# Some weight tiles stay whole float32 and are multiplied in two passes, and one stage's activations are issued later

## The chip, the cores and the metric

The kernel runs on one core of a Trainium2 chip. The metric is the device time of one execution in microseconds (us). The kernel before took 2136.09 us (median of three runs, 2128.08 to 2136.28).

## The reference

Two transformer blocks run one after the other on 256 tokens of width 1024, all in float32. The first block has a mixer of causal pooling and a chunked state-space recurrence, the second a gated linear recurrence beside a short convolution. Each block ends in a product-key expert layer ("peer"), cut here to what is computed:

```python
q = (hf @ w_query).reshape(T, PEER_HEADS, 2, D_KEY // 2)
s1 = jnp.einsum("thk,hnk->thn", q[:, :, 0], sub_keys1)
v1, i1 = lax.top_k(s1, PEER_TOPK)            # the same for s2
cand = v1[..., :, None] + v2[..., None, :]
top_s, pos = lax.top_k(cand.reshape(T, PEER_HEADS, -1), PEER_TOPK)
gates = jax.nn.softmax(top_s, axis=-1)
u = expert_down[ib]; v = expert_up[ib]       # 16384 experts, 128 chosen per token
out = einsum("thk,thkd->td", gates * gelu(einsum("td,thkd->thk", hb, u)), v)
```

The first mixer projects the modulated norm of x with `w_in` (25 tiles of 128 columns), mixes, and projects back with `w_out` (12 tiles).

## The kernel before

Tokens lie along the free dimension: activations are tiles of 128 features by 256 tokens. A weight tile is 128 x 8 x 128 float32 (512 KB) and gives one 128 x 256 product by eight steps over k. All 645 weight tiles pass through one planned list (`plan`), and SyncE fetches them in that order (`fetch_to`, "raw", three buffers).

To keep float32 precision with TensorE's one-pass format (fp32r), a tile is split in two: ScalarE casts it to the high part (`high`, L90, "whi"), VectorE subtracts that from the raw tile for the low part (`low`, L97, "wlo"). Activations are split in the same way (hh and hl, yh and yl). A product (`product_steps`, L124 to L126) is then three one-pass matmuls for each k: hi·hh, hi·hl and lo·hh, 24 in all. `take` splits the tiles up to two ahead (PREP = 2) of the one that is multiplied. Where a plain float32 matmul is called for (small ones such as the gates, L889), the program makes two passes out of each call.

The program order is written out by hand, engine by engine, and each engine works in that order:

- The first mixer (to about 209 us) starts with the modulation: rows of `w_ada` are multiplied by the conditioning vector on VectorE (L313, "aw"), scaled into h (`scaled`), and the first two `w_in` products run as a `pair`. A loop over the other 23 `w_in` tiles (L716) evacuates each product (`evac`: convolution, gates, pooling), runs a piece of the recurrence, and multiplies one more `aw` row. Then come eight `w_outs` and four `w_outp` tiles (`out`, `both`), with the residual on VectorE.
- Each peer layer starts with routing (to about 382 us in the first): 34 "S" tiles of expert_down and 16 query tiles are multiplied on TensorE, and behind each, a fixed ration (DRIP) of top-16 searches is put on VectorE. 
- Then the one-hot stage (`ahead`, `one_hots`; 398 to 570 us): 46 further expert_down tiles are multiplied beside 64 groups of float16 matmuls (L1317) that spread the gates over the experts. `beside` pulls 5 or 6 of a product's eight steps per group. ScalarE makes the gelu of a product (L1261, L1266), casts the weight tiles (L90) and copies the spread gates out of PSUM (L1291, L1292).
- Then the expert_up stage (to about 895 us): TensorE alone multiplies without a break. The second mixer and the second peer layer follow in the same way.

Of the kernel before, what the change touches and what calls it, by code (L numbers as in the profile page):

```python
# [8 lines left out]
F32 = _mybir.dt.float32  # L9
# [42 lines left out]
class Net:  # L52
# [16 lines left out]
    def plan(self, key, index, eng=None, spare=False):  # L69
        self.items.append([key, index, eng, None, spare])  # L70

    def fetch_to(self, n):
        while self.fetched < min(n, len(self.items)):
            it = self.items[self.fetched]
            it[3] = self.stream.tile([128, KT, 128], F32, name="raw", bufs=RAW)
            self.nc.sync.dma_start(it[3], self.a[it[0]][it[1]])
            self.fetched += 1

    def high(self, n):
# [4 lines left out]
        self.fetch_to(n + 1)  # L84
        if it[4]:
# [7 lines left out]
    def low(self, n):  # L93
        it = self.items[n]
        if len(it[3]) == 3:
            raw, hi, lo = it[3]
            (self.nc.gpsimd if it[2] == "pool" else self.nc.vector).tensor_sub(lo, raw, hi.bitcast(F32))  # L97
            it[3] = hi, lo
# [35 lines left out]
    def proj(self, key, index, xh, xl):  # L134
# [94 lines left out]
    def norm_steps(self, x, r, g, shift, wk):  # L229
# [3 lines left out]
        for k in range(KT + 1):  # L233
            if k < KT:
                t = wk.tile([128, T], F32, name="nt", bufs=3)
# [128 lines left out]

    def plan_mixer1(self):
        for n, i in enumerate(self.M1):
            self.plan("w_in", i, eng=None)
        for f in range(0, 8, 2):
            self.plan("w_outs", f)
            self.plan("w_outs", f + 1)  # L370
            self.plan("w_outp", f // 2)

    def mixer1(self, constants):
        tc, nc, a = self.tc, self.nc, self.a
        with self.sbuf("m1") as m1, self.sbuf("w1", 2) as wk, self.psum("q1", 3) as self.pp, self.psum("p1", 3) as px:
            xs = m1.tile([128, 8, T], F32, name="xs")
            self.scratch_in(m1)
# [4 lines left out]
            with self.sbuf("early") as self.ap:  # L382
# [30 lines left out]
                h = {}  # L413

                def scaled(k):
# [4 lines left out]
                    h[k] = self.ap.tile([128, T], F32, name="nt4", bufs=4)  # L420
                    if k < 6:
                        nc.scalar.activation(self.hh[:, k], xs[:, k], AF.Identity, scale=g[:, k:k + 1],
                                             bias=m[:, k:k + 1])
                        nc.scalar.activation(h[k], xs[:, k], AF.Identity, scale=g[:, k:k + 1], bias=m[:, k:k + 1])
                    else:
                        nc.vector.tensor_scalar(h[k], xs[:, k], g[:, k:k + 1], m[:, k:k + 1], op0=ALU.mult,
                                                op1=ALU.add)
                        nc.scalar.copy(self.hh[:, k], h[k])

                def rest(k):  # L430
                    nc.vector.tensor_sub(self.hl[:, k], h.pop(k), self.hh[:, k].bitcast(F32))  # L431
# [3 lines left out]
                rests = {4: (0, 1), 5: (2, 3), 6: (4, 5), 7: (6, 7)}  # L435
# [3 lines left out]
                both = self.pair(first, [("w_in", i) for i in self.M1[:2]], self.hh, self.hl, prep=1)  # L439
                for f in range(KT):  # L440
                    self.add_sum(self.square(self.x[:, f]), f)
                for k in range(KT):
# [18 lines left out]
                    for f in rests.get(k, ()):  # L461
                        rest(f)
# [4 lines left out]
                for _ in both:  # L467
                    pass

# [20 lines left out]
            yh = m1.tile([128, 12, T], F32R, name="yh")  # L490
            yl = m1.tile([128, 12, T], F32R, name="yl")
# [114 lines left out]
            def outputs(p):  # L606
# [13 lines left out]
                def gated():  # L620
# [4 lines left out]
                    def parts():  # L625
                        self.add_square(y, p)

                        gn = self.v("ssd_norm", p)
# [27 lines left out]
            def pool_out():  # L656
# [3 lines left out]
                t = wk.tile([128, T], F32, name="po", bufs=3)  # L660
# [938 lines left out]
```

## Time and profile before

| | us |
|---|---|
| median of 3 runs | 2136.09 (2128.08 to 2136.28) |
| the profiled execution, its own time | 2142.61 |
| span of its trace, first to last instruction | 2140.8 |
| TensorE busy, VectorE busy, ScalarE busy | 1996.0, 1581.2, 1099.2 |
| mean granted TensorE clock | 0.982 |

PE is the matmul stream, PEld the weight load beside it, DVE is VectorE, ACT ScalarE, POOL GpSimd, SP SyncE. The entry of a matmul is longer than the distance to the next, as matmuls overlap: what a matmul costs in a stream is read from start to start. The same holds on DVE by a smaller amount.

### The profile page before, as it was taken

Reading aid. Unit: us, or ns where it says so; the run is one execution under the profiler, and the core shown is the slowest. Engines: PE = TensorE matmul, PEld = TensorE weight load, DVE = VectorE, ACT = ScalarE, POOL = GpSimd, SP = SyncE. Lnnn points to the kernel's source line nnn. Section 1 sums busy time; section 2 is a strip of 40 time slices with the busy share of each in tenths; the row PEclk is TensorE's granted clock in tenths of the full one; section 3 lists DMA queues with packets and bytes.
Section 4 is the critical chain, followed back from the end, with each engine's and each line's share of the span. In section 5 each row is a group of like instructions: output and inputs, shape, how many; then the busy total and the mean of one; then the engine's idle time right before and its main releaser. Section 6 shows DMA issues by size and latency. Waiting matters only on the chain.

```text
span 2140.8 us, 41974 instructions
## 1 busy us (share of the span) xinstructions
PE 1996.0 (93%) x16976; PEld 1959.5 (92%) x16976; DVE 1581.2 (74%) x3061; ACT 1099.2 (51%) x2019; POOL 53.2 (2%) x52
## 2 busy tenths in 40 slices
PE   4888888999999999999999998889999999999998
PEld 4778888888999999999999998888889999999998
DVE  7998899888755555675678779998887555555555
ACT  4564444665544444444466554446655444444444
POOL 3021000000000000000000010000000000000000
PEclk6999999999999999999999999999999999999999
DMA  6755444433455555575545564444335555555553
GB/s 249 254 185 181 148 157 149 149 129 129 159 206 187 187 187 187 192 247 192 187 149 178 182 208 153 148 148 146 132 129 182 192 188 183 191 183 186 186 187 127
DMA packets 102724, 376.68 MB, mean 176 GB/s; under 512 B 11648, under 2 KB 12032, under 8 KB 101504
## 3 DMA queue, kind: packets, MB, share of 16 engines
q1 hardware_dynamic: 101520, 369.38, 49.9%
q0 software_dynamic: 576, 4.19, 0.5%
q8 instruction: 133, 2.18, 0.4%
q14 instruction: 63, 0.52, 0.1%
q10 hardware_dynamic: 432, 0.41, 0.1%
HBM read 370.80 MB, written 3.15 MB: 175 GB/s over the span
## 4 chain that ended last, share of the span: by engine, by line
PE 69%; DVE 20%; ACT 5%; issue 3%; DMA 2%; SPq 0%; DVEq 0%; ACTq 0%
PE acc L1361 10%; PE acc L1363 10%; PE acc L1362 10%; PE mm L126 8%; PE mm L125 8%; PE mm L124 8%; DVE wlo L97 6%; PE acc L124 3%; PE acc L125 3%; PE acc L126 3%; ACT whi L90 2%; DVE aw L313 2%; DMA aw<-in_w_ada_dram 2%; PE mm L1317 2%; PE sm L1317 2%
## 5 line engine op out<-in xcount | busy, mean ns | idle before, releaser
L97 DVE TENSOR_TENSOR wlo<-raw,whi 128x1024 fp32r<-128x1024 f32 x642 | 785.6, 1225 | 256.6 <-ACT whi L90 255.2
L90 ACT CAST whi<-raw 128x1024 fp32r<-128x1024 f32 x642 | 671.9, 1048 | 178.9 <-PE acc L1362 97.4
L126 PE MATMUL mm<-hh,wlo 128*128 128x256 f32 x2120 | 604.1, 285 | 38.7 <-DVE wlo L97 38.7
L124 PE MATMUL mm<-hh,whi 128*128 128x256 f32 x2120 | 604.6, 285 | 11.5 <-ACT whi L90 8.9
L125 PE MATMUL mm<-hl,whi 128*128 128x256 f32 x2120 | 600.0, 283 | 10.9 <-DVE hl L431 6.0
L1361 PE MATMUL acc<-wh,whi 128*128 128x256 f32 x2048 | 575.1, 281 | 2.9 <-DVE x L1471 2.1
L1362 PE MATMUL acc<-wl,whi 128*128 128x256 f32 x2048 | 574.1, 280 | 1.9 <-DVE wl L117 1.7
L1363 PE MATMUL acc<-wh,wlo 128*128 128x256 f32 x2048 | 573.5, 280 | 2.2 <-DVE wlo L97 2.2
L126 PEld LDWEIGHTS mm<-hh,wlo 128*128 128x128 f32 x2120 | 407.7, 192 | 48.5 <-DVE wlo L97 48.1
L124 PEld LDWEIGHTS mm<-hh,whi 128*128 128x128 f32 x2120 | 404.8, 191 | 15.4 <-ACT whi L90 10.1
L125 PEld LDWEIGHTS mm<-hl,whi 128*128 128x128 f32 x2120 | 406.3, 192 | 12.7 <-DVE hl L431 6.5
L1361 PEld LDWEIGHTS acc<-wh,whi 128*128 128x128 f32 x2048 | 385.9, 188 | 3.3 <-DVE x L1471 2.3
L1363 PEld LDWEIGHTS acc<-wh,wlo 128*128 128x128 f32 x2048 | 386.4, 189 | 2.6 <-DVE wlo L97 2.6
L1362 PEld LDWEIGHTS acc<-wl,whi 128*128 128x128 f32 x2048 | 385.0, 188 | 2.7 <-DVE wl L117 2.7
L116 ACT CAST wh<-X 128x256 fp32r<-128x256 f32 x256 | 103.4, 404 | 231.2 <-PE acc L1363 231.2
L124 PE MATMUL acc<-hh,whi 128*128 128x256 f32 x736 | 215.9, 293 | 0.0
L125 PE MATMUL acc<-hl,whi 128*128 128x256 f32 x736 | 205.0, 279 | 0.0
L126 PE MATMUL acc<-hh,wlo 128*128 128x256 f32 x736 | 204.5, 278 | 0.0
L117 DVE TENSOR_TENSOR wl<-X,wh 128x256 fp32r<-128x256 f32 x256 | 108.1, 422 | 90.9 <-ACT wh L116 90.9
L124 PEld LDWEIGHTS acc<-hh,whi 128*128 128x128 f32 x736 | 139.0, 189 | 0.0
L125 PEld LDWEIGHTS acc<-hl,whi 128*128 128x128 f32 x736 | 138.8, 189 | 0.0
L126 PEld LDWEIGHTS acc<-hh,wlo 128*128 128x128 f32 x736 | 138.3, 188 | 0.0
(345 smaller groups left out, 1970.4 us busy)
## 6 DMA issues: line engine op xcount, KB each, us to landing
raw<-in_down_dram SPq DMA_DIRECT2D x256, 512.0 KB, 3.2
raw<-in_up_dram SPq DMA_DIRECT2D x256, 512.0 KB, 3.8
raw<-in_w_in_dram SPq DMA_DIRECT2D x81, 512.0 KB, 3.3
aw<-in_w_ada_dram SPq DMA_DIRECT2D x48, 512.0 KB, 4.5
raw<-in_w_query_dram SPq DMA_DIRECT2D x32, 512.0 KB, 3.3
raw<-in_w_outs_dram SPq DMA_DIRECT2D x8, 512.0 KB, 3.8
raw<-in_w_out_dram SPq DMA_DIRECT2D x8, 512.0 KB, 4.1
raw<-in_w_outp_dram SPq DMA_DIRECT2D x4, 512.0 KB, 3.7
```

The costliest lines, as they stand in the source:

```text
L90: self.nc.scalar.copy(hi, it[3])
L97: (self.nc.gpsimd if it[2] == "pool" else self.nc.vector).tensor_sub(lo, raw, hi.bitcast(F32))
L116: self.nc.scalar.copy(hi, src)
L117: self.nc.vector.tensor_sub(lo, src, hi.bitcast(F32))
L124: nc.tensor.matmul(ps, hi[:, k], xh[:, k], start=k == 0 and clear, stop=False, skip_group_check=True)
L125: nc.tensor.matmul(ps, hi[:, k], xl[:, k], start=False, stop=False, skip_group_check=True)
L126: nc.tensor.matmul(ps, lo[:, k], xh[:, k], start=False, stop=k == KT - 1, skip_group_check=True)
L313: self.nc.vector.scalar_tensor_tensor(w, w, 1.0, self.crow, op0=ALU.mult, op1=ALU.mult, accum_out=self.mod[:, j:j + 1])
L1317: nc.tensor.matmul(pg[:, j], o2[j], o1[:, j // 2, b, :, j % 2], start=b == 0, stop=b == 1, skip_group_check=True)
L1361: nc.tensor.matmul(o, hi[:, d], wh, start=i == 0 and d < 4, stop=False, skip_group_check=True)
L1362: nc.tensor.matmul(o, hi[:, d], wl, start=False, stop=False, skip_group_check=True)
L1363: nc.tensor.matmul(o, lo[:, d], wh, start=False, stop=i == NK - 1, skip_group_check=True)
```

## The change

1. A planned tile can be "whole": `high` and `low` pass it by, and `product_steps` calls eight plain float32 matmuls of the raw tile with a float32 activation, two passes each. Whole tiles come from a ring of three buffers of their own ("rawf") or from the ring of the others ("shared").
2. In the first mixer, `w_in` tiles number 0, 1, 2, 4, 6, ... 16 in the order of multiplication (10 of 25) and all 12 output tiles are whole. The activations are kept in float32 (h and ys); hh and hl are made after the first pair, yh and yl are gone.
3. In each routing, ten S tiles (5, 8, ... 32) are whole. `norm_steps` also writes a float32 h, in the first peer layer with one more ScalarE instruction for each k.
4. In the one-hot stage, the gelu of a product is issued after step 3 of the next product, where it stood right behind its own.

```diff
@@ fetch_to, high
+            if it[2] == "own":
+                it[3] = self.whole.tile([128, KT, 128], F32, name="rawf", bufs=RAW)
+            else:
+                it[3] = self.stream.tile([128, KT, 128], F32, name="raw", bufs=RAW)
...
+        if it[2]:
+            it[3] = it[3],
+            return
@@ product_steps
-        hi, lo = self.take(key, index, prep)
+        w = self.take(key, index, prep)
+        if len(w) == 1:
+            for k in range(KT):
+                nc.tensor.matmul(ps, w[0][:, k], xh[:, k], start=k == 0 and clear, stop=k == KT - 1,
+                                 skip_group_check=True)
+                yield
+            return
+        hi, lo = w
@@ norm_steps
+                t = wk.tile([128, T], F32, name="nt", bufs=3) if whole is None or shift is not None else whole[:, k]
...
+                    if whole is not None:
+                        nc.scalar.activation(whole[:, k], t, AF.Identity, bias=shift[:, k:k + 1])
@@ plan_mixer1
+        return n < 2 or n % 2 == 0 and n < 18
...
-            self.plan("w_in", i, eng=None)
+            self.plan("w_in", i, whole=self.unsplit(n) and "own")
...
+            self.plan("w_outs", f, whole="own")
+            self.plan("w_outs", f + 1, whole="shared")
+            self.plan("w_outp", f // 2, whole="own" if f % 4 else "shared")
@@ mixer1, modulation
-                both = self.pair(first, [("w_in", i) for i in self.M1[:2]], self.hh, self.hl, prep=1)
+                both = self.pair(first, [("w_in", i) for i in self.M1[:2]], h, None, prep=1)
...
-                    for f in rests.get(k, ()):
-                        rest(f)
...
+                for k in range(KT):
+                    nc.scalar.copy(self.hh[:, k], h[:, k])
+                for k in range(KT):
+                    nc.vector.tensor_sub(self.hl[:, k], h[:, k], self.hh[:, k].bitcast(F32))
@@ mixer1, recurrence
-                        nc.scalar.mul(yh[:, 4 + p], y, gn)
-                        post.append(lambda: nc.vector.scalar_tensor_tensor(
-                            yl[:, 4 + p], y, gn, yh[:, 4 + p].bitcast(F32), op0=ALU.mult, op1=ALU.subtract))
+                        nc.scalar.mul(ys[:, 4 + p], y, self.v("ssd_norm", p))
@@ mixer1, output
-                        nc.tensor.matmul(o, hi[:, kk], yh[:, k], start=False, stop=False, skip_group_check=True)
-                        nc.tensor.matmul(o, hi[:, kk], yl[:, k], start=False, stop=False, skip_group_check=True)
-                        nc.tensor.matmul(o, lo[:, kk], yh[:, k], start=False, stop=k == 3, skip_group_check=True)
+                        nc.tensor.matmul(ps[f][:, 1], w[:, 4 * b + k], ys[:, k], start=False, stop=k == 3,
+                                         skip_group_check=True)
@@ plan_peer, peer
+                self.plan(down, st[1], whole=4 < st[1] < N0 and st[1] % 3 == 2 and "own")
...
+                return self.proj(down, i, *([h] if self.items[self.taken][2] else [self.hh, self.hl]))
@@ peer, one-hot stage
+                            for k, _ in enumerate(product(ps, i, clear=slot < 4)):
+                                if k == 3 and done:
+                                    activated(*done)
+                                yield
+                            done = kind, i, ps, o
+                        activated(*done)
```

VectorE in the loop over the `w_in` tiles, before: "wlo" is the subtraction for a weight tile, "cva" the convolution, "xs" its gate, "aw" a modulation row.

```order
111 L97 TENSOR_TENSOR wlo<-raw,whi 128x1024
112 L359 SCALAR_TENSOR_TENSOR cva<-mm,hcw,cva 128x255
...
115 L679 SCALAR_TENSOR_TENSOR xs<-th,cva 128x256
116 L313 SCALAR_TENSOR_TENSOR aw,mod<-aw,crow 128x1024
117 L97 TENSOR_TENSOR wlo<-raw,whi 128x1024
118 L359 SCALAR_TENSOR_TENSOR cva<-mm,hcw,cva 128x255
...
121 L679 SCALAR_TENSOR_TENSOR xs<-th,cva 128x256
122 L547 TENSOR_TENSOR cbt<-aux,U 128x512
123 L313 SCALAR_TENSOR_TENSOR aw,mod<-aw,crow 128x1024
124 L97 TENSOR_TENSOR wlo<-raw,whi 128x1024
```

The same place now (every line of the program has another number, as the file grew).

```order
104 L103 TENSOR_TENSOR wlo<-raw,whi 128x1024
105 L374 SCALAR_TENSOR_TENSOR cva<-mm,hcw,cva 128x255
...
108 L682 SCALAR_TENSOR_TENSOR xs<-th,cva 128x256
109 L560 TENSOR_TENSOR cbt<-aux,U 128x512
110 L328 SCALAR_TENSOR_TENSOR aw,mod<-aw,crow 128x1024
111 L374 SCALAR_TENSOR_TENSOR cva<-mm,hcw,cva 128x255
...
114 L682 SCALAR_TENSOR_TENSOR xs<-th,cva 128x256
...
117 L328 SCALAR_TENSOR_TENSOR aw,mod<-aw,crow 128x1024
118 L103 TENSOR_TENSOR wlo<-raw,whi 128x1024
```

Between the two `aw` rows the subtraction is gone; it stands in every second turn of the loop.

ScalarE in the one-hot stage, before: "X<-acc" and "act<-acc" are the two halves of a gelu, "X<-mm" and "X<-sm" the copies of spread gates, "whi" the cast of a weight tile.

```order
325 L1214 ACTIVATE oh_4682<-cst,kI_2199 128x128 x2
326 L1261 ACTIVATE X_2466<-acc_2203 128x236
327 L1266 ACTIVATE act<-acc_2203 128x20
328 L90 CAST whi<-raw 128x1024
329 L1291 ACTIVATE X_2466<-sm 128x26x4
330 L1292 ACTIVATE X_4413<-sm 128x64x4
```

The same stage now.

```order
312 L1211 ACTIVATE oh_4188<-cst,kI_1734 128x128 x2
313 L96 CAST whi<-raw 128x1024
314 L1297 ACTIVATE X_2010<-sm 128x24x4
315 L1298 ACTIVATE X_3757<-sm 128x64x4
316 L1211 ACTIVATE oh_4188<-cst,kI_1734 128x128 x2
317 L1259 ACTIVATE X_2010<-acc_1737 128x216
318 L1264 ACTIVATE act<-acc_1737 128x40
```

The cast stands ahead of the gelu of the product before it, and the copies of a group can come ahead of that gelu.

## Rows read from the trace of the kernel before

**Rows 1.** Windows by stage: us; PE, PEld, DVE, ACT, POOL busy; clock; DMA, GB/s

```profile
0.00:47.00 47.00, 18.83 (x90) 16.53 (x91) 36.35 (x82) 19.67 (x38) 18.86 (x15) 0.66 0.73 268
47.00:139.00 92.00, 83.11 (x658) 76.55 (x658) 87.84 (x172) 56.31 (x122) 2.31 (x4) 0.97 0.65 236
139.00:167.00 28.00, 18.83 (x139) 17.38 (x138) 26.30 (x46) 11.23 (x22) 10.19 (x9) 0.88 0.37 132
167.00:209.00 42.00, 35.31 (x291) 33.92 (x291) 38.05 (x80) 19.16 (x33) 8.73 (x8) 1.00 0.47 168
240.00:382.00 142.00, 124.96 (x1014) 120.96 (x1013) 141.04 (x479) 62.42 (x101) 0.00 (x0) 0.98 0.43 149
398.00:570.00 172.00, 158.19 (x1533) 153.48 (x1532) 144.73 (x262) 106.49 (x292) 0.00 (x0) 1.00 0.38 132
1284.00:1430.00 146.00, 126.07 (x1043) 121.62 (x1043) 139.96 (x483) 65.52 (x106) 0.00 (x0) 1.00 0.43 151
1640.00:2120.00 480.00, 480.00 (x4078) 480.00 (x4077) 278.57 (x346) 228.76 (x340) 0.54 (x1) 1.00 0.55 188
```

**Rows 2.** TensorE timeline: start, us, line, operation, idle; split products at the two clocks

```profile
1111.95 0.28 PE L126 MATMUL mm<-hh,wlo 128*128 128x256 f32 x1
...
1113.90 0.28 PE L125 MATMUL mm<-hl,whi 128*128 128x256 f32 x1
...
37.60 0.41 PE L125 MATMUL mm<-hl,whi 128*128 128x256 f32 x1
...
41.23 0.41 PE L124 MATMUL mm<-hh,whi 128*128 128x256 f32 x1
```

**Rows 3.** The gates' plain float32 matmuls (L889): one chain, then all 32 passes

```profile
1114.47 1.03 PE L889 MATMUL aux<-xc,wg 128*128 128x256 f32 x4
...
L889 PE MATMUL aux<-xc,wg x32: 378/379/454, 1110.8 to 1137.0; 128*128 128x256 f32 x32
```

**Rows 4.** VectorE timeline, one turn of the `w_in` loop

```profile
76.15 1.22 DVE L97 TENSOR_TENSOR wlo<-raw,whi 128x1024 fp32r<-128x1024 f32 x1
77.28 1.51 DVE L359 SCALAR_TENSOR_TENSOR cva<-mm,hcw,cva 128x255 f32<-128x255 f32 x3
...
79.04 1.22 DVE L313 SCALAR_TENSOR_TENSOR aw<-aw,crow 128x1024 f32<-128x1024 f32 x1
...
80.19 1.22 DVE L97 TENSOR_TENSOR wlo<-raw,whi 128x1024 fp32r<-128x1024 f32 x1
```

**Rows 5.** VectorE timeline, the end of the modulation

```profile
29.57 1.73 DVE L97 TENSOR_TENSOR wlo<-raw,whi 128x1024 fp32r<-128x1024 f32 x1
...
45.82 0.98 DVE L431 TENSOR_TENSOR hl<-nt,hh 128x256 fp32r<-128x256 f32 x2
...
49.65 0.48 DVE L359 SCALAR_TENSOR_TENSOR cva<-mm,hcw,cva 128x255 f32<-128x255 f32 x1 [2.52 <-ACT cva L357]
```

**Rows 6.** VectorE timeline, the end of the recurrence

```profile
162.68 0.48 DVE L630 SCALAR_TENSOR_TENSOR yl<-yo,vecs,yh 128x256 fp32r<-128x256 f32 x1
163.08 0.41 DVE L666 TENSOR_TENSOR yl<-po,yh 128x256 fp32r<-128x256 f32 x1
```

**Rows 7.** TensorE timeline: the first output product behind the pair, the next norm's sum

```profile
166.75 0.36 PE L758 MATMUL mm<-yh,whi 128*128 128x256 f32 x1
...
207.46 0.61 PE L224 MATMUL sm<-ones,ns 128*128 128x1 f32 x4 [1.62 <-POOL ns L219]
```

**Rows 8.** Waits in 240 to 382, then 1290 to 1440: us, times, longest

```profile
PE mm L126 <- DVE wlo L97: 15.9, 16, 1.9
...
PE mm L126 <- DVE wlo L97: 18.0, 17, 1.9
```

**Rows 9.** Waits in 398 to 570, the first one-hot stage

```profile
ACT X L1261 <- PE acc L126: 40.8, 27, 2.5
...
PE sm L1317 <- ACT X L1292: 6.3, 12, 0.9
...
PE mm L1317 <- ACT X L1292: 5.1, 9, 0.9
```

More of the change, by code (lines that the diff above doesn't have):

```diff
@@ L66, in psum, with plan @@
         return self.tc.tile_pool(name=name, bufs=bufs, space=PSUM, reuse_waits="tile")
-    def plan(self, key, index, eng=None, spare=False):
-        self.items.append([key, index, eng, None, spare])
+    def plan(self, key, index, whole=False, spare=False):
+        self.items.append([key, index, whole, None, spare])
     def fetch_to(self, n):
@@ L227, in total_sum, with norm_steps @@
         return ps
-    def norm_steps(self, x, r, g, shift, wk):
+    def norm_steps(self, x, r, g, shift, wk, whole=None):
         nc = self.nc
@@ L749, in out @@
                 q = ps[f] = self.pp.tile([128, 2, T], F32, name="mm")
-                self.product(q[:, 0], "w_outs", f, yh[:, 4:], yl[:, 4:])
+                self.product(q[:, 0], "w_outs", f, ys[:, 4:], None)
             def both(j):
-                hi, lo = self.take("w_outp", j)
+                w, = self.take("w_outp", j)
                 for b in range(2):
@@ L795, in mixer1 @@
                 ps[f] = self.pp.tile([128, 2, T], F32, name="mm")
-            two = self.pair([ps[0][:, 0], ps[1][:, 0]], [("w_outs", 0), ("w_outs", 1)], yh[:, 4:], yl[:, 4:])
+            two = self.pair([ps[0][:, 0], ps[1][:, 0]], [("w_outs", 0), ("w_outs", 1)], ys[:, 4:], None)
             for _ in range(KT - 2):
@@ L1063, in S @@
             def S(i):
-                return self.proj(down, i, self.hh, self.hl)
+                return self.proj(down, i, *([h] if self.items[self.taken][2] else [self.hh, self.hl]))
             with self.sbuf("rt") as rt:
+                self.whole = rt
+                h = rt.tile([128, KT, T], F32, name="h")
                 kt = rt.tile([128, 16, 128], F32, name="keys")
@@ L1118, in peer @@
                 nc.sync.dma_start(kt, a[keys])
-                norm = self.norm_steps(self.x, row, g, shift, rt)
+                norm = self.norm_steps(self.x, row, g, shift, rt, h)
                 next(norm)
@@ L1250, in product, with activated @@
                             yield
+                    def activated(kind, i, ps, o):
+                        nonlocal there
+                        if kind == "H":
+                            held[i] = ps
+                        elif kind == "R":
+                            acts[i] = o
+                            nc.scalar.activation(o, ps, gelu)
+                        else:
+                            t1 = t0 + 4 if t0 else 0
+                            nc.scalar.activation(o[:, t1:], ps[:, t1:], gelu)
+                            if not t0:
+                                there += 1
+                                return
+                            t = og.tile([128, 192], F32, name="act", bufs=2)[:, :t1]
+                            nc.scalar.activation(t, ps[:, :t1], gelu)
+                            first.append((t1, o[:, :t1], t))
```

79 lines of the change are left out of this document (19 added, 60 removed).

## The prediction

> **What bounds the kernel now.** I read the windows by stage first [rows 1], since the mean over the span says little here: TensorE is busy 480.00 of 480 us in the second expert_up stage, and there no tile changes. The changed stages look different. In the loop of the first mixer (47 to 139 us) VectorE is busy 87.84 of 92 us, in the two routings 141.04 of 142 and 139.96 of 146. TensorE is behind it there: the waits say that in the routings it stood still for a weight tile's low part 15.9 and 18.0 us [rows 8]. VectorE is the bound of these stages, and the subtraction for a weight tile is a large part of its work: one turn of the loop is 4.04 us from one subtraction to the next, of which the subtraction takes 1.13 (76.15 to 77.28) [rows 4]. In the one-hot stage neither is full (TensorE 158.19 and VectorE 144.73 of 172 us) [rows 1]; ScalarE waits there 40.8 us for the product whose gelu is next, and TensorE in turn 6.3 + 5.1 us for ScalarE's copies [rows 9].
>
> **What a whole tile costs.** A split product runs 17 steps in 1113.90 - 1111.95 = 1.95 us, 0.1147 each, so 24 take 2.75 us [rows 2]. A plain float32 matmul is two passes; four of them span 1.03 us, the last one's own entry is 0.378, so three steps take 0.65: 0.217 each [rows 3]. A whole tile has 16: 3.47 us, 0.72 more than a split one. It saves VectorE 1.13 us, and ScalarE the cast. So it is a trade of 1.13 on one engine against 0.72 on another, and pays only where VectorE is the one that is late. No stretch of 16 passes stands in the trace: from below I bound a pass by 0.1147 (it can't be shorter than a one-pass matmul), from above by its whole entry, 0.378; I take 0.217, the nearest row, of the same shape.
>
> The Trainium skill's "FP8 and Floating Point Precision", section "TensorE Precision Notes", speaks against the change: true float32 takes four passes through the array. By that, 32 passes stand against 24, and a whole tile would be 4/3 of 2.75, 3.67 us, an estimate; the trace shows two entries, each of nearly twice a one-pass matmul [rows 2, 3], so 3.8 rather than four. By the page the ten output tiles below would take 2 us more, and the sum would be 2094.
>
> **The first mixer, step by step.**
> Modulation (to 47 us). Three subtractions go (the first took 1.73 us, the others 1.1 each) and eight of hl, two of which have an entry of 0.98 us, move behind the pair; the last h can so be ready about 6 us earlier, and the loop's first convolution, which waited 2.52 us until 49.65 [rows 5], follows it. The moved hl work fills that idle time. Against it stands the clock: it was 0.66 in this stage [rows 1], and at the lower of the two levels, 1.2 GHz, the same 17 steps took 41.23 - 37.60 = 3.63 us, almost twice as long [rows 2]; a whole tile is then some 6.6 us instead of 3.5, and tile 2 may run so. I take -5, with -2 and -7 as ends.
>
> Loop (47 to 139 us). Whole tiles 4, 6, ... 16 take away seven subtractions: 7 x 1.13 = -7.9. TensorE gets 7 x 0.72 = 5 us more; its 658 instructions at 0.1147 make 75 of 92 us, so 17 were free and it stays behind VectorE. -8.
>
> End of the recurrence (139 to 167 us). Three subtractions for output tiles go (3.4 us) and twelve of yl: eight at 0.40 (162.68 to 163.08) and four at 0.34, 4.6 us [rows 6]. VectorE was busy 26.30 of 28 us, but TensorE and GpSimd (busy 18.83 and 10.19 us) [rows 1] hand it the last products, the pooling and the sum of squares here, and one of these can be late next. Of 8.0 I take -6, the ends -4 and -8.
>
> Output tiles (167 to 209 us). Here the trade turns. From the first product behind the pair (166.75) to the next norm's sum (207.46) [rows 7] are 40.7 us, with ten products: 27.5 us of TensorE before, 34.7 now. Nine subtractions (10.2 us) leave VectorE's 38.05, so TensorE becomes the bound: 34.7, the spread norm 0.5 and the residual, its square and GpSimd's addition behind the last product, some 4 us, make about 40. I take 0, with +4 and -3 as ends. Taking their turn here are also the fetches: a whole tile's buffer comes free when TensorE has read it, not when VectorE has, and SyncE's later fetches (the next query tiles) queue behind that. Six tiles are in flight, some 20 us, and the DMA engines were 0.47 busy [rows 1], so I price this at nothing; with less cover it would show as ScalarE waiting for raw tiles.
>
> Norm before the first routing: eight more ScalarE instructions of about 0.3 us in a chain that TensorE waits for: +1 (0 to 2.5).
>
> **The routings.** Ten subtractions less in each is 11.3 us on VectorE; TensorE gets 7.2 us more and loses at most its waits for low parts, 15.9 and 18.0 [rows 8], a net 8.7 and 10.8. As both engines end up nearly level and the ration of searches is uneven from step to step, neither limit is reached: -8 each, ends -3 and -11.
>
> **The one-hot stages.** ScalarE no longer stands before an unfinished product, where the copies and the cast queued up behind its gelu and TensorE behind the copies. What TensorE lost to that is 11.4 us in the first stage [rows 9]. The cast is now immediately ahead of the gelu, and a group that ends between them waits for both, so I count half: -5 each, ends 0 and -11. VectorE, at 144.73 of 172 us [rows 1], allows it.
>
> Sum: -5 - 8 - 6 + 0 + 1 - 16 - 10 = -44 us. From the profiled execution's own 2142.61 that is 2098.6; that execution lies 6.5 us above the median of the runs, 2136.09, so I forecast 2092.
>
> **Rivals.**
> TensorE takes over in the routings too. For it: its need there, 142 - 15.9 + 7.2 = 133.3 us, against VectorE's 141.0 - 11.3 = 129.7: it is already the larger. Against it: it has two split tiles of lead over VectorE. If unevenness eats most of the gain (-2 each) and the output tiles cost 4: -44 + 12 + 4 = -28, 2108.
> The delayed gelu brings nothing: the stall moves from the gelu to the cast. For it: ScalarE's work in a group is the same, 106.49 us in 172 [rows 1]. Then -34: 2102.
> VectorE stays the bound all through: the whole 11.3 twice, 8 in the recurrence, 11 in each one-hot stage: about -69, 2067.
> Slower: in a long stream of plain passes the weight load isn't hidden, and a pass costs its whole entry, 0.378 [rows 3]. A whole tile is then 6.05 us, 3.3 above a split one. The routings would get 33 us more on TensorE, which had 17 to spare (142 - 124.96) [rows 1]: +16 each; the ten output tiles 60.5 and a tail of 4 against 40.7: +24; the loop 23 against 17 spare: +6; with -5 and -10 as before, +47: 2183. It decides from about 0.27 a pass on, where the routings stop gaining. Against it: chains of four already run at 0.217.
>
> **How the numbers follow.** 0.5% of 2136, 11 us, is what a measurement of this kernel can tell from no change. The forecast gets 0.50, TensorE in the routings 0.22, of which 0.05 for a gain under 11 us, the useless delay 0.15, VectorE throughout 0.06, slower 0.05, and 0.02 that some wait I don't see eats it all. So faster 0.88, the same 0.07, slower 0.05. The good ends of the terms together with VectorE throughout give about 2066, the bad ends without the slower case (-2, -8, -4, +4, +2, -6, 0) make -14, 2122; as they won't all fall together I take 2068 to 2116.
>
> **What would show it.** The plain products should step at 0.217. The subtractions for weight tiles should number 42 fewer; 47 to 139 us should shrink by about 8 and TensorE's wait for low parts in the routings to a few us, while VectorE falls below 0.97 busy there. In the one-hot stage ScalarE's wait for the product should be mostly gone and TensorE's for the copies halved. Were a routing not shorter by at least 3 us, or the output tiles longer by more than 5, the forecast would be wrong in that step.

## The result: 57 us less, and the profile after

| | before | after |
|---|---|---|
| median (lowest to highest) of 4 runs each, us | 2132.19 (2128.08 to 2136.28) | 2074.80 (2073.15 to 2077.16) |
| ratio, with its 95% interval | | 0.9725 (0.9704 to 0.9746) |
| the profiled execution, its own time | 2142.61 | 2077.16 |
| span of its trace | 2140.8 | 2075.4 |

The change is worth 57 us by the medians and 65 us between the two profiled executions. The 8 us between these are not the change's: the profiled execution of before lies 10 us above the median of its runs, that of after 2 us.

To see where the time went I took the same pieces of work in both traces as landmarks and compared the time between them: the first convolution of the loop on VectorE, the VectorE instruction that reads a norm's sum ("re"), the first and the last score of a routing on TensorE, the transpose of the chosen keys behind it, the first and the last group of spread gates, SyncE's last store.

```
stretch                                     before    after     step    forecast
start to the first convolution               49.65    44.19     -5.5       -5
  to the norm's sum behind the recurrence   117.27   103.61    -13.7    -8 and -6
  to the next norm's sum (output tiles)      42.13    39.85     -2.3        0
  to the first score of routing 1            23.55    24.38     +0.8       +1
routing 1, to the last score                125.62   119.09     -6.5   }
  from there to the keys                     22.36    17.94     -4.4   }   -8
  to the first group of gates                10.23    10.96     +0.7
one-hot stage 1, first to last group        168.96   158.20    -10.8       -5
expert_up 1, to the second mixer's norm     521.2    517.7      -3.5        0
second mixer and its output                 213.6    214.2      +0.6        0
routing 2, to the last score                126.38   119.50     -6.9   }
  from there to the keys                     22.29    17.93     -4.4   }   -8
  to the first group of gates                10.22    10.96     +0.7
one-hot stage 2                             169.01   158.19    -10.8       -5
expert_up 2, to the last store              515.42   515.41      0.0        0
```

The windows after, cut at the same pieces of work as [rows 1] (us; PE, PEld, DVE, ACT, POOL busy; clock; DMA, GB/s):

```profile
0.00:42.00 42.00, 20.98 (x86) 17.20 (x87) 31.67 (x73) 15.83 (x35) 17.89 (x15) 0.72 0.75 282
42.00:122.00 80.00, 78.35 (x539) 69.64 (x538) 76.52 (x157) 45.22 (x104) 2.22 (x2) 1.00 0.76 277
122.00:148.00 26.00, 23.00 (x165) 20.56 (x164) 23.55 (x45) 10.30 (x25) 10.82 (x11) 1.00 0.43 156
148.00:188.00 40.00, 40.00 (x207) 35.91 (x206) 28.11 (x72) 11.07 (x24) 7.98 (x8) 1.00 0.51 180
212.00:350.00 138.00, 133.73 (x984) 128.83 (x985) 133.98 (x492) 56.81 (x101) 0.00 (x0) 0.98 0.44 157
367.00:528.00 161.00, 156.16 (x1534) 152.57 (x1532) 143.35 (x261) 106.11 (x294) 0.00 (x0) 1.00 0.41 142
1238.00:1378.00 140.00, 132.69 (x994) 127.59 (x993) 132.41 (x486) 55.67 (x97) 0.00 (x0) 0.99 0.47 168
```

In the loop (42 to 122 us) and the routings TensorE and VectorE are now equally full; in the output stage (148 to 188) TensorE is busy 40.00 of 40 us and VectorE only 28.11, where VectorE was the fuller [rows 1].

A whole tile costs what the four-pass chain [rows 3] had told. Two of the long streams on TensorE's timeline (start, us, line, operation):

```profile
151.60 3.62 PE L131 MATMUL mm<-ys,rawf 128*128 128x256 f32 x16
233.69 3.62 PE L131 MATMUL mm<-h,rawf 128*128 128x256 f32 x16
```

Sixteen passes span 3.62; without the last one's own entry, 0.378, fifteen steps take 3.24: 0.216 each, 3.46 us a tile. The weight loads are hidden, so the slower rival has no ground.

VectorE in the loop, where [rows 4] had a subtraction in every turn:

```profile
67.48 1.22 DVE L328 SCALAR_TENSOR_TENSOR aw<-aw,crow 128x1024 f32<-128x1024 f32 x1
...
68.63 1.51 DVE L374 SCALAR_TENSOR_TENSOR cva<-mm,hcw,cva 128x255 f32<-128x255 f32 x3
...
70.39 1.22 DVE L328 SCALAR_TENSOR_TENSOR aw<-aw,crow 128x1024 f32<-128x1024 f32 x1
...
71.53 1.22 DVE L103 TENSOR_TENSOR wlo<-raw,whi 128x1024 fp32r<-128x1024 f32 x1
72.67 1.51 DVE L374 SCALAR_TENSOR_TENSOR cva<-mm,hcw,cva 128x255 f32<-128x255 f32 x3
```

A turn without a subtraction goes from `aw` to `aw` in 70.39 - 67.48 = 2.91 us, and no row has an idle time before it: VectorE sets the pace of this turn. The end of the modulation, to be set beside [rows 5]:

```profile
40.19 2.76 DVE L483 TENSOR_TENSOR hl<-ys,hh 128x256 fp32r<-128x256 f32 x8
...
44.19 1.00 DVE L374 SCALAR_TENSOR_TENSOR cva<-mm,hcw,cva 128x255 f32<-128x255 f32 x2 [0.91 <-ACT cva L372]
```

The eight moved hl instructions stand where VectorE had waited 2.52 us; 0.91 us of waiting is left, and the convolution is 5.5 us earlier. No run takes back the two whole tiles of the pair, so how these 5.5 us divide is argued from the rows; only tile 2's share, 1.3 us, is measured below. The waits in the two routings, 218 to 350 and 1240 to 1380 us (us, times, longest), against [rows 8]:

```profile
PE mm L139 <- DVE wlo L103: 3.9, 4, 1.9
...
PE mm L139 <- DVE wlo L103: 3.7, 3, 1.9
```

The low parts cost TensorE 3.9 and 3.7 us in place of 15.9 and 18.0. And those of the first one-hot stage, 360 to 530 us, against [rows 9]:

```profile
ACT whi L96 <- PE acc L138: 49.4, 39, 2.3
...
PE sm L1323 <- ACT X L1298: 1.8, 6, 0.4
PE mm L1323 <- ACT X L1298: 1.8, 5, 0.4
```

ScalarE no longer waits for the gelu's product (40.8 us before), but now its cast (L96) waits, 49.4 us. TensorE's waits for the copies fell from 6.3 + 5.1 to 1.8 + 1.8 us.

### The profile page after: what moved, and what is told of

The parts are those of the page before. It is cut to its first block, busy times and chain, and to the rows that moved or that the text cites. A ratio compares the mean times of both kernels' runs of the same rounds, so it can differ in the third digit from the quotient of the medians.

```text
span 2075.4 us, 41216 instructions
## 1 busy us (share of the span) xinstructions
PE 2003.8 (97%) x16640; PEld 1959.9 (94%) x16640; DVE 1527.2 (74%) x3007; ACT 1055.8 (51%) x1983; POOL 52.0 (3%) x52
## 4 chain that ended last, share of the span: by engine, by line
PE 78%; DVE 15%; ACT 3%; issue 3%; DMA 1%; SPq 0%; DVEq 0%; ACTq 0%
PE acc L1367 11%; PE acc L1369 11%; PE acc L1368 11%; PE mm L139 8%; PE mm L137 8%; PE mm L138 8%; PE acc L137 4%; PE acc L138 4%; DVE wlo L103 4%; PE acc L139 3%; PE mm L131 2%; PE mm L1323 2%; DVE aw L328 2%; PE sm L1323 2%; ACT whi L96 1%
## 5 line engine op out<-in xcount | busy, mean ns | idle before, releaser
L103 DVE TENSOR_TENSOR wlo<-raw,whi 128x1024 fp32r<-128x1024 f32 x600 | 733.9, 1224 | 251.2 <-ACT whi L96 249.4
L96 ACT CAST whi<-raw 128x1024 fp32r<-128x1024 f32 x600 | 627.8, 1047 | 245.8 <-PE acc L138 107.4
L139 PE MATMUL mm<-hh,wlo 128*128 128x256 f32 x1880 | 531.8, 283 | 10.8 <-DVE wlo L103 10.6
L137 PE MATMUL mm<-hh,whi 128*128 128x256 f32 x1880 | 537.8, 286 | 2.3 <-ACT X L1130 1.4
L138 PE MATMUL mm<-hl,whi 128*128 128x256 f32 x1880 | 531.2, 283 | 4.9 <-DVE hl L260 2.7
L139 PEld LDWEIGHTS mm<-hh,wlo 128*128 128x128 f32 x1880 | 360.6, 192 | 13.6 <-DVE wlo L103 13.4
L138 PEld LDWEIGHTS mm<-hl,whi 128*128 128x128 f32 x1880 | 357.9, 190 | 6.5 <-DVE hl L260 3.2
L137 PEld LDWEIGHTS mm<-hh,whi 128*128 128x128 f32 x1880 | 356.2, 189 | 5.5 <-ACT X L1130 1.6
```

What stands on the lines that cost most here:

```text
L96: self.nc.scalar.copy(hi, it[3])
L103: self.nc.vector.tensor_sub(lo, raw, hi.bitcast(F32))
L137: nc.tensor.matmul(ps, hi[:, k], xh[:, k], start=k == 0 and clear, stop=False, skip_group_check=True)
L138: nc.tensor.matmul(ps, hi[:, k], xl[:, k], start=False, stop=False, skip_group_check=True)
L139: nc.tensor.matmul(ps, lo[:, k], xh[:, k], start=False, stop=k == KT - 1, skip_group_check=True)
```

## The experiments

Of the twelve runs ten are edits of the changed kernel, one repeats such an edit, and one is the changed kernel unaltered. Times of one comparison share the runs of the kernel before on one chip; those runs differ from chip to chip (medians 2132 to 2143), so I give the ratios, and read each step between landmarks of the traces. By its ratio the changed kernel itself would take 2075, 2079, 2081 and 2084 us beside the four comparisons. Two executions of one program differ by up to 1.3 us in some stretches, and by 5 us in an expert_up stage (the last experiment). The stretch of the second mixer, too, is 4 us and more shorter than in the changed kernel's first profile in some runs whose edits lie elsewhere. So a step of a few us is read from the stage that has the edit, not from the total.

### The routings without whole tiles

```diff
-                self.plan(down, st[1], whole=4 < st[1] < N0 and st[1] % 3 == 2 and "own")
+                self.plan(down, st[1], whole=False)
...
-                norm = self.norm_steps(self.x, row, g, shift, rt, h)
+                norm = self.norm_steps(self.x, row, g, shift, rt)
```

> As the changed kernel, but all routing tiles are split again (the float32 h of the norms is gone too). Theory: every subtraction taken out of the routing counted in full, because VectorE alone set its pace; the two routings (first score to keys) were 10.95 and 11.2 us shorter, so this gives back 22 us: 2097. By the prediction's -8 each: 2091. Rival, TensorE's longer whole tiles ate most of it and the routings became shorter through what came earlier: under 8 us, below 2083.

Measured: 2092.63 us, ratio 0.9818 (0.9804 to 0.9832). The routings grow by 6.6 + 4.3 = 10.9 and 6.8 + 4.5 = 11.3 us, and the norm ahead of routing 1 is 0.7 shorter, as only the high and low parts of h are written. The waits in 218 to 360 us of this kernel:

```profile
PE mm L139 <- DVE wlo L103: 17.9, 18, 1.9
```

The medians give less, 18 us against the 2075 of this comparison: in this execution the stretch of the second mixer and the two expert_up stages, which the edit leaves as they are, are 5.5, 1.1 and 3.3 us shorter. By the stages, every one of the ten subtractions counts in full (10 x 1.13 = 11.3), and TensorE's wait for low parts comes back. Its cover was larger than the 7.2 us that the whole tiles cost it.

### Nineteen whole tiles in each routing

```diff
-                ... st[1] % 3 == 2 and "own")
+                ... st[1] % 3 > 0 and "own")
```

> As the changed kernel, but 20 tiles of each routing are whole (5, 7, 8, 10, 11, ... 32) instead of 10. Theory: TensorE is busy 133.7 of 138 us there already, so ten more at 0.72 us add 7.2 and can win back at most its remaining wait for low parts, 3.9: +3 to +7 a routing, 2081 to 2089, with that wait near zero and VectorE well under 0.9 busy. Rival, each further whole tile takes 1.1 us off as the first ten did: 2053.

The edit makes nineteen tiles whole (5, 7, 8, 10, 11, ... 32), not the twenty that the expectation counts: nine more than the change.

Measured: 2078.15 us, ratio 0.9737 (0.9721 to 0.9754). To the last score the routings grow by 2.6 and 4.7 us; from there to the keys they shrink by 1.6 and 1.5. That is +1.1 and +3.2 net, where the theory had +3 to +7; the direction is the theory's, and the rival's further gain is out. The windows of this kernel, 212 to 333 (up to the last scores) and 333 to 350, and then of the changed kernel, 331 to 349:

```profile
212.00:333.00 121.00, 117.85 (x797) 111.41 (x798) 110.36 (x428) 41.28 (x81) 0.00 (x0) 0.99 0.43 152
333.00:350.00 17.00, 17.00 (x105) 15.69 (x104) 13.79 (x56) 7.14 (x11) 0.00 (x0) 1.00 0.53 194
```

```profile
331.00:349.00 18.00, 15.94 (x118) 14.91 (x116) 17.77 (x65) 7.89 (x12) 0.00 (x0) 1.00 0.41 147
```

With ten whole tiles VectorE is full in a routing's end (17.77 of 18) and TensorE not; with nineteen TensorE is (17.00 of 17), and in the longer part before it the nine subtractions less buy nothing. The ten of the change stand near the point where the bound changes hands.

### More whole tiles in a routing's end alone

```diff
-                ... st[1] % 3 == 2 and "own")
+                ... st[1] % 3 > (0 if st[1] > 23 else 1) and "own")
```

> The changed kernel with more whole tiles in the routings, but only late: up to tile 23 every third (6 of them) as now, from tile 24 on two of three (7 instead of 3 or 4). With 20 whole tiles all through, the time to the last score grew (TensorE became the bound there) and that from the last score to the keys fell by 1.5 us. Theory, VectorE paces the end of a routing and TensorE its beginning: the end's 1.5 us can be had alone, -1.5 us in each routing, 2072. Rival, TensorE is the bound from tile 24 on too: +1 to +2 in each, 2078.

From tile 24 on the edit makes six tiles whole (25, 26, 28, 29, 31, 32) in place of three; up to 23 they are seven (5, 8, ... 23), as in the change. The expectation miscounts both.

Measured: 2073.41 us, ratio 0.9695 (0.9679 to 0.971). From the last score to the keys 1.6 and 1.5 us less, before it 0.3 and 1.1 more. The first theory holds for the end; net it is 1.3 and 0.4 us, less than the runs can tell, and seen in the traces only.

### Output tiles split again

Here the three plan lines, `product`, and the yh and yl of the recurrence are as in the kernel before (L758, L630, L666 there); h has a buffer of its own, as ys is gone.

```diff
-            self.plan("w_outs", f, whole="own")
-            self.plan("w_outs", f + 1, whole="shared")
-            self.plan("w_outp", f // 2, whole="own" if f % 4 else "shared")
+            self.plan("w_outs", f)
+            self.plan("w_outs", f + 1)
+            self.plan("w_outp", f // 2)
```

> As the changed kernel, but the 12 output tiles of the first mixer and their activations are split again. Theory: whole output tiles help before the output products, where VectorE is late (about 8 us from the loop to the norm's root), and bring nothing among the products themselves, which TensorE now bounds (from the root to the next norm's: the same within 3 us): 2083 to 2086. Rival, what they save on VectorE they cost on TensorE: 2075.

Measured: 2086.93 us, ratio 0.978 (0.9766 to 0.9793). +7.5 us up to the norm's sum behind the recurrence, +2.5 from there to the next norm's sum, +2.4 to the first score; of the last, 1.2 us lies within what this stretch differs by in the other runs (24.4 to 25.6), the rest I can't place. So the end of the recurrence gave nearly the whole 8.0 us that VectorE was spared there, and the output tiles did not cost but gave 2.5.

### The loop's tiles split again

```diff
-        return n < 2 or n % 2 == 0 and n < 18
+        return n < 2
```

> The changed kernel with the eight tiles number 2, 4, ... 16 of w_in split again (tiles 0 and 1 and all output tiles stay whole). Theory, VectorE paces the loop: eight subtractions of 1.13 us come back, +9 us up to the end of the recurrence, nothing behind it, 2084. Rival, a part of the eight is hidden in VectorE's idle 5%: +5, 2080. Rival, TensorE gives back 8 x 0.7 us of its own: +3, 2078.

Measured: 2079.30 us, ratio 0.9726 (0.9712 to 0.9741); by that alone nothing would have changed. But the runs of this kernel lie 12 us apart (2070.06 to 2082.43), and in its profiled execution the two expert_up stages and the second mixer, which have no edit, are 6.3, 5.2 and 3.5 us shorter than in the changed kernel (the last section shows of what kind that is). So the stage decides: the trace has +8.3 us at the norm's sum behind the recurrence and nothing from there to the next sum. Of the 8.3, 1.3 stand ahead of the first convolution, where the subtraction for tile 2 comes back, and 6.9 behind it. The granted clock fell to 0.93 in 42 to 130 us of this execution, but VectorE was busy 85.69 of these 88 us, so that can hold little of it. VectorE's turns have their subtraction again:

```profile
72.10 1.22 DVE L103 TENSOR_TENSOR wlo<-raw,whi 128x1024 fp32r<-128x1024 f32 x1
...
76.13 1.22 DVE L103 TENSOR_TENSOR wlo<-raw,whi 128x1024 fp32r<-128x1024 f32 x1
```

4.03 us from one to the next, as in [rows 4]. The first theory holds. From the first convolution to the norm's sum, this experiment's 6.9 and the 7.5 of the one before make 14.4, where the change as a whole gave 13.7 and the forecast's two terms 14: the parts very nearly add up.

### The gelu at once again

```diff
-                            for k, _ in enumerate(product(ps, i, clear=slot < 4)):
-                                if k == 3 and done:
-                                    activated(*done)
-                                yield
-                            done = kind, i, ps, o
+                            yield from product(ps, i, clear=slot < 4)
+                            activated(kind, i, ps, o)
```

> As the changed kernel, but the gelu of a product stands right behind its product again in the one-hot stages. Theory: the whole 10.8 us by which each one-hot stage became shorter comes from the delay, so 2096, with ScalarE's wait for the product back at some 40 us a stage. By the prediction's half: 2085. Rival, the stages are shorter because they start with other buffers ahead: 2075.

Measured: 2091.14 us, ratio 0.9804 (0.9783 to 0.9826). The one-hot stages grow by 10.6 and 10.6 us; nothing else moves by more than the executions differ (the expert_up stages are 2.0 and 4.7 us shorter, so the median is 16 us above 2075 and not 21). ScalarE's wait for the product whose gelu is next is back, 41.0 us in 368 to 540 us. So all of the one-hot stages' gain is the gelu's, and the rival of other buffers is out.

To see how, I read TensorE's loss at each of the 64 groups: the start of the group's first matmul less the start of the matmul before it, less 0.115 for that matmul's own step, sorted by how many of its eight steps the product under way had done when the group came (first stage, mean us at a group; the second has the same within 0.2 in the sum):

```
steps done          0     1     2     3     4     5   6, 7   sum of all groups
groups              9     7     9     8     8     9    14
before              0   0.69  0.27  0.93  0.43  0.08    0         18.9
after               0   0     0     0.53  0.36  0.05    0          7.7
gelu at once        0   0.69  0.27  0.91  0.41  0.09    0         18.7
gelu after step 1   0   0     0.26  0.92  0.45  0.08    0         14.2
cast after step 5   0   0     0     0     0     0       0          0.3
gelu at once,
  cast after 5      0   0.69  0.27  0.05  0.02  0       0          7.9
```

The second group follows the first with no product step between them, so the matmul before it is the last of the first group's eight. Counted from the first of the eight, as the sums in the expectations below are, every sum is 0.4 larger (8.1 and 0.7 there for 7.7 and 0.3 here); the differences are the same.

The mean loss goes with the place; at one place the groups still differ (0 to 0.68 us at 4 steps done in the first stage before). The last rows are the next three experiments.

### The gelu after step 1

```diff
-                                if k == 3 and done:
+                                if k == 1 and done:
```

> The changed kernel with one edit: in the one-hot stage the gelu of a product is issued after step 1 of the next product, not after step 3. Theory of the position: a group of spread gates loses time when its copies stand on ScalarE behind an instruction that waits for the unfinished product. In the changed kernel TensorE loses some 0.5 us at groups that start 3 or 4 steps into a product (behind the cast), none at those that start 1 or 2 steps in. With the gelu after step 1, the groups 2 steps in must lose their 0.3 us again and those 3 steps in 0.8, as they did with the gelu at once: about +4 to +5 us in each one-hot stage, 2083 in all. Rival, any delay is as good: no change, 2075.

Measured: 2088.41 us, ratio 0.9767 (0.9753 to 0.9781). The one-hot stages grow by 6.5 and 6.5 us, somewhat more than the 4 to 5 expected, with the loss back at groups 2 and 3 steps in and none at those 1 step in, as the theory said. The rival is out: a delay helps only for the groups that it lets pass.

### The cast after step 5

```diff
                     def product(ps, i, **kw):
                         for k, _ in enumerate(self.product_steps(ps, down, i, self.hh, self.hl, prep=1, **kw)):
-                            if k == 2:
+                            if k == 5:
```

> The changed kernel with one edit: in the one-hot stage the cast of the next but one weight tile is issued after step 5 of a product, where it stood after step 2, ahead of the gelu; the gelu stays after step 3. Theory: what TensorE still loses there (7.3 us in each stage, at the groups that start 3 or 4 steps into a product) is the copies' wait behind a cast that stands at the head of ScalarE until the product before has been read. With the cast behind step 5 that loss goes: -5 to -7 us in each stage, 2061 to 2065 in all. Rival A, ScalarE's amount of work is what is late: no change, 2075. Rival B, the cast comes too late for VectorE's subtraction: TensorE waits for the low part instead, 2075 to 2085.

Measured: 2059.62 us, ratio 0.9641 (0.9625 to 0.9657). The one-hot stages shrink by 6.9 and 6.7 us. The median is 19 us below the 2079 of this comparison, under the range expected; the expert_up stages, without an edit, are 4.3 and 5.2 us shorter in this execution (the last experiment takes that up). ScalarE's timeline in the changed kernel, and in this one:

```profile
434.42 1.05 ACT L96 CAST whi<-raw 128x1024 fp32r<-128x1024 f32 x1 [0.73 <-PE acc L138]
435.37 0.28 ACT L1259 ACTIVATE X<-acc 128x140 f32<-128x140 f32 x1
435.55 0.26 ACT L1264 ACTIVATE act<-acc 128x116 f32<-128x116 f32 x1
435.70 0.20 ACT L1297 ACTIVATE X<-sm 128x40 f32<-128x40 f32 x1
435.78 0.40 ACT L1298 ACTIVATE X<-sm 128x256 f32<-128x256 f32 x1
```

```profile
431.19 0.29 ACT L1259 ACTIVATE X<-acc 128x140 f32<-128x140 f32 x1 [0.62 <-PE acc L139]
431.38 0.26 ACT L1264 ACTIVATE act<-acc 128x116 f32<-128x116 f32 x1
431.52 1.05 ACT L96 CAST whi<-raw 128x1024 fp32r<-128x1024 f32 x1
432.46 0.21 ACT L1297 ACTIVATE X<-sm 128x40 f32<-128x40 f32 x1
```

In the first, ScalarE stands 0.73 us before a cast that waits for the product before, then needs 1.3 us for cast and gelu, and the copies come behind all of it. In the second the wait is before the gelu, with the cast behind it and no wait of its own. The waits in 360 to 530 us of the changed kernel had two rows of TensorE for ScalarE's copies, 3.6 us together; here none is left of the one-hot stage, only that for the first weight tile of the stage behind, which the changed kernel has too:

```profile
PE acc L1369 <- DVE wlo L103: 1.1, 1, 1.1
```

ScalarE's amount of work is the same, so rival A falls, and with no low part waited for in the stage, rival B too.

### The gelu at once with the cast after step 5

```diff
-                            if k == 2:
+                            if k == 5:
...
-                                if k == 3 and done:
-                                    activated(*done)
+                            yield from product(ps, i, clear=slot < 4)
+                            activated(kind, i, ps, o)
```

> The changed kernel with the gelu of a product at once again, right behind its last step, and the cast after step 5. Theory of the position: what TensorE loses at a group belongs to the instruction that stands ahead of its copies; the gelu at once costs 0.69 and 0.27 us at groups 1 and 2 steps into a product (7 and 9 of them), 7.3 us in a stage, and the cast the rest. So the loss is about 7 to 8 us in each one-hot stage, as in the changed kernel (8.1): the two edits would be worth about the same each, no change within 1 us a stage. Rival, the gelu's delay is what counts and the cast matters only behind it: the loss is 15 us or more, +7 in each stage.

Measured: 2075.73 us, ratio 0.9703 (0.9671 to 0.9736); the one-hot stages last as in the changed kernel, to +0.1 us. The rival is out. Either edit alone takes away 11 us of the loss, and both together 18.6: groups 1 and 2 steps in belong to the gelu, those 3 and 4 in to the cast, each partly shared while both stand there.

### The changed kernel once more, and the best version

The first is the changed kernel unaltered, so that the others of this comparison stand beside it.

> The changed kernel, unaltered, beside the two that follow. In two of the experiments the expert_up stages, which no edit touches, were 4 to 5 us shorter, with TensorE's step from one matmul to the next at 0.1157 us on average over some 200 us where it is 0.1178 otherwise. Theory, this comes from execution to execution whatever the kernel: the stages up to the end of each one-hot stage last as long as before to within 1 us, and the expert_up stages may differ by up to 5 us each. Rival, the edits caused it: 515.4 us from the end of the second one-hot stage to the end, as in the first profile.

Measured: 2077.74 us (2068.42 to 2079.34), ratio 0.9714 (0.968 to 0.9747). All stages are as in the first profile to within 1.3 us, the expert_up stages too (515.4 again), so this run doesn't decide between theory and rival; its runs alone, 11 us apart, speak for the theory.

The best version has both edits that gained, the cast after step 5 and the later whole tiles.

> The changed kernel with both edits that gained: the cast of the one-hot stage after step 5 of a product (there TensorE's loss at the groups fell from 8.1 to 0.7 us in each stage), and in the routings two of three tiles whole from tile 24 on. They lie in different stages, so they should add up: -7 us in each one-hot stage and -1 in each routing, 16 us less than the unaltered changed kernel of the same comparison, 2058 to 2062.

Measured: 2060.44 us (2056.54 to 2061.0), ratio 0.9637 (0.9606 to 0.9667), 17 us below the changed kernel beside it and 79 below the kernel before. The end of the second one-hot stage is 16.0 us earlier than in the changed kernel: 6.9 and 6.9 in the one-hot stages, 1.3 and 0.5 in the routings, and the rest in stretches that no edit touches.

### The cast after step 5, a second time

> The kernel with the cast after step 5, unaltered, a second time. In its first profile both expert_up stages were shorter than the changed kernel's (4.2 and 5.2 us), with TensorE's mean step at 0.1157 us in the first 230 us of each. Theory, the step is set from execution to execution: a second profile may have 0.1178 there, and stages of the changed kernel's length. Rival, the edit brings it about: 0.1157 again in both stages, and 510.2 us from the last group of the second one-hot stage to the end. In both cases the one-hot stages are 6.7 to 6.9 us shorter than the changed kernel's, as the first time.

Measured: 2065.12 us, ratio 0.9639 (0.9623 to 0.9655). The one-hot stages are again 6.9 and 6.9 us shorter than the changed kernel's. But the second expert_up stage takes 515.4 us, where the first execution of the same program took 510.2. Windows of its first 130 us, in the first execution and in this one:

```profile
1552.00:1682.00 130.00, 130.00 (x1126) 130.00 (x1125) 77.53 (x100) 62.62 (x93) 0.54 (x1) 1.00 0.58 201
```

```profile
1557.00:1687.00 130.00, 130.00 (x1107) 130.00 (x1106) 75.96 (x99) 61.38 (x92) 0.54 (x1) 1.00 0.61 201
```

1126 matmuls in 130 us against 1107, with nothing idle and the granted clock 1.00 in both: the theory holds, this differs between executions and is no part of any edit.

## Why the prediction was right, and which steps were mis-sized

The direction and the mechanism were right: VectorE was late, and a subtraction taken away there paid until TensorE was level with it. The time, 2074.8, lies in the range, 17 us below the 2092 forecast. Between the profiled executions the stretches up to the last store sum to -65.8, where the terms made -44. That the medians fell by no more than 57 is the scatter of the executions and no merit of the forecast: every stage of weight was forecast too small but the loop. Of the signs named ahead, the subtractions are 42 fewer (600 against 642); VectorE's busy share in the routings, which was to fall below 0.97, is 0.97 and 0.95. Step by step:

**The whole tile.** 3.47 us forecast from a chain of four, 3.46 measured. By the four passes that the Trainium skill's "FP8 and Floating Point Precision", section "TensorE Precision Notes", gives for float32 it would be 3.67, an estimate; measured it is 3.46 / (8 x 0.1147) = 3.8 one-pass steps for each k, and the measurement decides.

**Modulation, norm.** -5 and +1 forecast, -5.5 and +0.8 measured; the first experiment shows the float32 h behind the second.

**Loop and end of the recurrence.** -8 and -6, measured -13.7 together; taken back one at a time, 6.9 for the loop's seven tiles and 7.5 for the end of the recurrence. The forecast did not weigh that the granted clock of the last part was 0.88 before [rows 1] and is 1.00 now, and no run holds the clock still. It can have given little: VectorE was busy 26.30 of those 28 us, so all that it can have waited there is 1.7.

**Output tiles.** "TensorE becomes the bound" was right: it is busy 40.00 of 40 us there. My 40 us were nearly its size: between the two instructions of [rows 7], which were 40.7 us apart, it is 39.4 now:

```profile
147.63 3.70 PE L760 MATMUL mm<-ys,raw 128*128 128x256 f32 x16
...
187.01 0.50 PE L237 MATMUL sm<-ones,ns 128*128 128x1 f32 x4
```

I took the 0.7 that this forecast as 0, and 1.3 came. From one norm's sum to the next on VectorE it is 2.3, as the second sum was read 1.6 us behind TensorE's instruction before (207.46 to 209.05) and is read 0.6 behind it now (187.01 to 187.65).

**Routings.** "Neither limit is reached: -8 each" was mis-sized: -10.9 and -11.3, the limit of VectorE. The rival that saw TensorE take over had the right amount of work for it (133.3 us; 133.73 are busy now), but the two engines overlap well enough that TensorE waits only 3.9 us. The bound does change hands, past ten tiles, as the run with nineteen shows.

**One-hot stages.** "So I count half: -5 each" is the step that failed most: -10.8 each. Half was the right idea, of the wrong whole. I took TensorE's loss from the wait rows, 11.4 us; from start to start it was 18.9. TensorE's timeline of before, at a group of the second stage, shows why:

```profile
1461.48 0.28 PE L126 MATMUL acc<-hh,wlo 128*128 128x256 f32 x1
1461.95 0.62 PE L1317 MATMUL mm<-og,oh 128*128 128x128 f16 x8 [0.19 <-ACT X L1292]
```

The group starts 0.47 us after the matmul before it, whose step is 0.115: 0.355 lost. The row gives 0.19, for it counts from the end of that matmul's entry (0.28 long, which is the 0.165 missing), and a loss under 0.165 has no row. The Trainium skill's "Perfetto Trace Analysis", section "Tensor Engine Instruction (MATMUL, LD_WEIGHTS)", says that the end of a matmul in a profile is computed, not observed; the two rows agree, as the entry ends 0.165 after the next matmul of a stream would have started. The 21 waits of [rows 9] were each short by that, 3.5 us, and smaller ones were absent. Two more rows of the same stage, for VectorE's part of the copies, I left out:

```profile
PE mm L1317 <- DVE X L1295: 1.3, 3, 0.8
PE sm L1317 <- DVE X L1295: 0.4, 2, 0.2
```

Of the 18.9 the delayed gelu took 11.2, 59%; what the cast kept, as the forecast had said of groups between the two, is 7.7, of which the later cast then left 0.3.

**The rivals.** Of the four, "VectorE stays the bound all through" came nearest, in its terms too (11.3 in each routing, 11 in each one-hot stage), though I gave it 0.06. Its sum is wrong: with the other terms as forecast these make -65 and 2071, not -69 and 2067. The slower rival's +47 leaves out the -6 and +1 of the terms that it does not touch. "The delayed gelu brings nothing" and "TensorE takes over in the routings" are out by the runs that undo each part, the slower one by the step of 0.216.

**Not accounted for.** The first expert_up stage is 3.5 us shorter though nothing in it changed; two executions of one program differ there by 5 us, so I leave it with that scatter.

## What to carry to other kernels

Where two engines share a step, moving a piece of work from the late one to the other was worth its whole length here until the other was level; nearly doubling the dose then showed at once where that point is. On an engine that works in order, look at what stands at the head of its queue waiting when somebody else needs the small thing behind it: both times it paid to issue the instruction later, nearer to where its own input is there (the cast three steps later was worth as much as the gelu's delay). Price a stall on TensorE from start to start, not by the idle time of its rows.

## What the runs showed of the hardware

In a stream of split products without a gap TensorE's mean step from matmul to matmul isn't one number. In the last 200 us of the second expert_up stage it is 0.1178 us in the profiles of all runs. In the first 230 us of both stages it was 0.1157 in the first execution with the later cast and 0.1178 in the second, at a granted clock of 1.00 in both (the rows above: 130 / 1126 and 130 / 1107 us, a little less, as a window also counts the matmuls that began just before it). Three further runs (the routings without whole tiles, the loop's tiles split, the gelu at once) had 0.1157 in the second stage alone. In the kernel with the loop's tiles split it was 0.1133 from 940 to 1020 us and again from 1100 to 1200. It holds over a whole stretch and then changes, and is worth some 5 us in a stage; what selects it no run here shows. A part of the scatter between executions of one kernel (2068.4 to 2079.3 us for the changed one) may be this.
